# Modulation vectors for the third and fourth layer: from accumulating matmuls on TensorE to running sums on VectorE

## The chip, the cores and the metric

The kernel runs on one core of one Trainium2 chip. Its engines are TensorE (PE, with its weight loads as PEld), VectorE (DVE), ScalarE (ACT), GpSimd (POOL) and SyncE (SP), which issues the loads and stores here. Each engine works through its own list of instructions in order and waits at the head of the list. The metric is the device time of one execution in microseconds; lower is better.

## The reference

A stack of four layers works on 512 tokens (256 context tokens and 256 latent tokens) with 1,024 features in fp32. Each layer has a token mixer (gated DeltaNet, S5, RWKV-7, gated DeltaNet) and then a SwiGLU feed-forward network (FFN). Before each of them stands an RMSNorm whose result is shifted and scaled, and behind each a gate. These shifts, scales and gates are six vectors of 1,024 numbers per layer, made from the conditioning vector `c` (latent tokens) and from `c_ctx` (context tokens):

```
for each layer l, each part p of 6:
    mod[l, p] = silu(cond) @ mod_w[l][:, p] + mod_b[l, p]      # cond is c_ctx and c: two rows
h = rmsnorm(x, w) * (1 + scale) + shift
x = x + gate * mixer_or_ffn(h)
swiglu(h) = (silu(h @ w_in[:, :2816]) * (h @ w_in[:, 2816:])) @ w_out
```

One part takes a product of a 2 x 1,024 matrix with a 1,024 x 1,024 matrix of weights (4 MB), so the work is mostly that of reading the weights. Six parts per layer are 24 MB.

## The kernel before

**Layout.** Features lie on the 128 partitions in 8 blocks (`KD = 8`), tokens along the free dimension (`T = 512`), and the residual stream `X` stays on chip. Every large product is made of three matmuls (`mm3`, L134 to L138): weight and activation are both split into a high and a low part in a rounded fp32 form, `whi`, `wlo`, `hhi`, `hlo`. A weight tile comes in as `wraw` (256 KB, SP), ACT makes `whi` of it by a cast (L129), DVE makes `wlo = wraw - whi` (L130). Each of the three has four buffers (`weights`, `bufs=4`); a tile of 128 x 512 holds four blocks of 128, thus it serves 12 matmuls.

**The FFN** (`ffn`, L243) first runs `norm`: ACT squares `X`, DVE adds up `acc` (L197), one matmul with `ones` sums it over the partitions (L202), ACT makes the root (L203, L204), DVE multiplies (`t`, L219), ACT applies shift and scale (L227) and makes `hhi` (L159), and DVE makes `hlo` (L160). Then come 22 rounds `f` of two dense products of 24 matmuls each, `g` into a bank of `psd` and `u` into a bank of `psw`; ACT takes the SiLU of `g`, DVE multiplies it by `u` (L260), and the product is split into `fh` (ACT) and `fl` (DVE). Then come 8 output rows of 66 matmuls each, whose result DVE adds to `X` (`residual`, L239).

**The lanes.** The modulation vectors of the next layer are made inside the FFN of the layer ahead. A `Lane` (class at L1197) holds a generator and a rate; at each of 68 calls of `tick` (two in a round `f`, three in an output row) it is moved on by so many steps. `mods` (L163) has 8 steps per part: in step `k` two 256 KB tiles `mraw` are loaded (SP, L170, three buffers) and four matmuls follow (L172), with `cs` (128 x 32, in which two columns are in use) as weights and 256 columns of `mraw` as the moving operand; each goes to its own group of 32 partitions of the bank `psm`, and the 8 steps accumulate there. Then DVE copies the bank's half (L177), two transposes bring the vector onto the partitions (L180), and DVE adds the bias (L184). The lane takes 48 steps in 58 ticks. A second lane, `s5_prep`, runs in the first FFN alone.

**What sets the order.** The program is written in one order, but a scheduler that simulates the engines puts each engine's list into its final order when the kernel is built: work that is ready in its simulation is moved ahead of work that is not. So the ticks set a priority, and the place in an engine's list is only known from the built program.

Of the kernel before, what the change touches and what calls it, by code (L numbers as in the profile page):

```python
# [12 lines left out]
F32 = mybir.dt.float32  # L13
F32R = mybir.dt.float32r
AF = mybir.ActivationFunctionType
ALU = mybir.AluOpType
# [3 lines left out]
P = 128  # L20
T = 512
HALF = 256
KD = 8
# [4 lines left out]
class Net:  # L28
# [134 lines left out]
    def mods(self, l, parts, pool, raw):  # L163
        nc = self.nc
        for part in parts:
# [18 lines left out]
            nc.vector.tensor_tensor(dst, src, b, op=ALU.add)  # L184
            yield

    def raw_tile(self, pool, tag="mraw", bufs=4):
        return lambda: pool.tile([P, T], F32, name=self.nm(tag), tag=tag, bufs=bufs)

# [53 lines left out]
    def ffn(self, l, ts=slice(0, T), nxt=None):  # L243
        nc, tc = self.nc, self.tc
        with self.weights(), self.banks(w=4, m=2), self.open_h(), \
                tc.tile_pool(name=f"ffn{l}", bufs=1, reuse_waits="tile") as fp:
            if nxt is not None:
                self.lanes.append(Lane(self.mods(nxt, range(6), "m", self.raw_tile(fp, bufs=3)), 48, 58))
            if nxt == 1:
                self.lanes.append(Lane(self.s5_prep(fp, "m"), 130, 60))  # L250
            self.norm(l, 1, ts)
            hi, lo = [], []
            for f in range(NFFN):
                g = self.dense8(self.d["ffnin"][l, f, 0], ts)
                self.tick()
                u = self.dense8(self.d["ffnin"][l, f, 1], ts, pool="w")
                s = self.tmp()
                self.last_act = nc.scalar.activation(s[:, ts], g[:, ts], AF.Silu)
                a = self.tmp()
                nc.vector.tensor_tensor(a[:, ts], s[:, ts], u[:, ts], op=ALU.mult)  # L260
                ah = fp.tile([P, T], F32R, name=self.nm("fh"), tag=f"fh{f}")
                al = fp.tile([P, T], F32R, name=self.nm("fl"), tag=f"fl{f}")
                self.split(a[:, ts], ah[:, ts], al[:, ts])
                hi.append(ah)
                lo.append(al)
                self.tick()
            for f in range(KD):
                ps = self.ps("d")
                for k0 in range(0, NFFN, 8):
                    n = min(8, NFFN - k0)  # L270
                    w = self.wtile(self.d["ffnout"][l, f][:, k0 * P:(k0 + n) * P])
                    for i in range(n):
                        k = k0 + i
                        self.mm3(ps[:, ts], *w[i], hi[k][:, ts], lo[k][:, ts], k == 0, k == NFFN - 1)
                    self.tick()
                self.residual(l, 5, f, ps, ts)
            self.drain()
# [1588 lines left out]
```

## Time and profile before

| | |
|---|---|
| time, median of three runs | 3986.14 us (3984.36 to 4014.93) |
| the profiled execution: its time, its span | 3998.94 us, 3997.2 us |
| busy share of the span | PE 91%, PEld 70%, DVE 65%, ACT 51%, POOL 6% |
| granted clock of TensorE over the span | 0.928 of full speed |

The page gives busy time per engine, the chain of work that ended last (71% of it on PE), and groups of instructions by line of the kernel. A group names the output and inputs by the program's names, so `psm<-mraw,cs` is a matmul of a modulation step. The second FFN lies at about 1508 to 1931 us of the span and the third at about 2738 to 3153 us, in the trace's time axis; RWKV lies between them and the last GDN mixer behind the third. In a timeline the first number is the start, the second the duration. A matmul's record is longer than the distance to the next one's start, because matmuls are pipelined; what one costs is read from the starts. An fp32 matmul leaves two records, so that `x8` in an L172 row are four matmuls.

### The profile page before, as it was taken

To read this page: it belongs to the slowest core of one execution; us is meant where nothing else is said; L and a number is where in the kernel's file an instruction comes from. 1 tells how busy PE (TensorE), PEld (TensorE's weight loads), DVE (VectorE), ACT (ScalarE), POOL (GpSimd) and SP (SyncE) were. 2 spreads that over 40 slices of the span, in tenths; PEclk is the share of its full clock that TensorE was granted. 3 is DMA by queue.
4 is the path that set the end of the run, shared out by engine and by line. 5 is a ranking of instruction groups with operands and counts; after the bars stand their busy time and mean duration, and the time that the engine had idled before them with its cause. 6 is when DMAs were issued, how large, how long until landed. Compare 5 with 4: busy or idle time off the path is not lost.

```text
span 3997.2 us, 79365 instructions
## 1 busy us (share of the span) xinstructions
PE 3617.7 (91%) x30954; PEld 2803.3 (70%) x30954; DVE 2598.3 (65%) x6026; ACT 2053.7 (51%) x4533; POOL 238.9 (6%) x352
## 2 busy tenths in 40 slices
PE   6899999989999798999768999998999889998899
PEld 3676777757777686777546666675777667877798
DVE  6777888677776744333775677655332487888665
ACT  5666777553332334232454465544232467777654
POOL 0000000022322200000000000000000000000000
PEclk8999999989999898999877799868999898899899
DMA  5222111146665623444375456502444211121155
GB/s 194 93 83 80 49 46 49 46 127 192 201 213 179 240 86 124 156 154 144 131 274 199 143 197 210 185 12 95 156 155 157 71 54 44 61 64 61 57 178 161
DMA packets 266104, 511.62 MB, mean 128 GB/s; under 512 B 30464, under 2 KB 55680, under 8 KB 263296
## 3 DMA queue, kind: packets, MB, share of 16 engines
q1 hardware_dynamic: 265728, 506.55, 38.7%
q8 instruction: 243, 3.98, 0.4%
q14 instruction: 133, 1.09, 0.1%
HBM read 454.27 MB, written 52.17 MB: 127 GB/s over the span
## 4 chain that ended last, share of the span: by engine, by line
PE 71%; DVE 10%; ACT 9%; DMA 6%; issue 3%; SPq 0%; POOL 0%; DVEq 0%; ACTq 0%
PE psd L136 11%; PE psd L137 10%; PE psd L138 9%; PE psw L136 8%; PE psw L137 7%; PE psw L138 7%; PE psm L172 2%; DMA vx<-rw_x 2%; DMA mraw<-in_modw 2%; PE psi L530 2%; PE psw L1581 1%; PE psc L1390 1%; PE pso L1402 1%; PE psc L1407 1%; DMA wraw<-in_rwkv_rkv 1%
## 5 line engine op out<-in xcount | busy, mean ns | idle before, releaser
L129 ACT CAST whi<-wraw 128x512 fp32r<-128x512 f32 x854 | 521.5, 613 | 973.8 <-PE psd L137 553.6
L130 DVE TENSOR_TENSOR wlo<-wraw,whi 128x512 fp32r<-128x512 f32 x854 | 581.9, 683 | 643.6 <-ACT whi L129 629.1
L136 PE MATMUL psw<-hhi,whi 128*128 128x512 f32 (+1 forms) x1536 | 587.2, 382 | 19.3 <-ACT kT L372 6.5
L138 PE MATMUL psw<-hhi,wlo 128*128 128x512 f32 (+1 forms) x1536 | 570.9, 372 | 0.0
L137 PE MATMUL psw<-hlo,whi 128*128 128x512 f32 (+1 forms) x1536 | 570.8, 372 | 0.0
L136 PEld LDWEIGHTS psw<-hhi,whi 128*128 128x128 f32 x1536 | 296.2, 193 | 92.4 <-ACT whi L129 11.5
L138 PEld LDWEIGHTS psw<-hhi,wlo 128*128 128x128 f32 x1536 | 294.9, 192 | 50.5 <-issue 2.1
L137 PEld LDWEIGHTS psw<-hlo,whi 128*128 128x128 f32 x1536 | 295.6, 192 | 45.6 <-issue 2.5
L136 PE MATMUL psd<-hhi,whi 128*128 128x512 f32 (+1 forms) x784 | 296.7, 378 | 16.4 <-ACT hhi L159 16.4
L137 PE MATMUL psd<-hlo,whi 128*128 128x512 f32 (+1 forms) x784 | 290.3, 370 | 0.0
L138 PE MATMUL psd<-hhi,wlo 128*128 128x512 f32 (+1 forms) x784 | 289.1, 369 | 0.0
L136 PE MATMUL psd<-fh,whi 128*128 128x512 f32 (+1 forms) x704 | 261.4, 371 | 0.0
L137 PE MATMUL psd<-fl,whi 128*128 128x512 f32 (+1 forms) x704 | 257.4, 366 | 0.0
L138 PE MATMUL psd<-fh,wlo 128*128 128x512 f32 (+1 forms) x704 | 256.8, 365 | 0.0
L239 DVE SCALAR_TENSOR_TENSOR X<-psd,modT,X 128x256 f32<-128x256 f32 x376 | 166.6, 478 | 83.2 <-PE psd L138 81.0
L136 PEld LDWEIGHTS psd<-hhi,whi 128*128 128x128 f32 x784 | 149.4, 191 | 63.8 <-ACT hhi L159 19.8
L172 PE MATMUL psm<-mraw,cs 128*32 128x256 f32 x1280 | 139.2, 410 | 34.1 <-DMA mraw<-in_modw 21.7
L137 PEld LDWEIGHTS psd<-hlo,whi 128*128 128x128 f32 x784 | 149.0, 190 | 29.0 <-issue 2.9
L138 PEld LDWEIGHTS psd<-hhi,wlo 128*128 128x128 f32 x784 | 149.1, 190 | 24.1 <-issue 0.4
L136 PEld LDWEIGHTS psd<-fh,whi 128*128 128x128 f32 x704 | 132.9, 189 | 34.4 <-ACT whi L129 11.1
L137 PEld LDWEIGHTS psd<-fl,whi 128*128 128x128 f32 x704 | 133.0, 189 | 21.7 <-issue 1.6
L138 PEld LDWEIGHTS psd<-fh,wlo 128*128 128x128 f32 x704 | 133.0, 189 | 21.7
(537 smaller groups left out, 7778.9 us busy)
## 6 DMA issues: line engine op xcount, KB each, us to landing
mraw<-in_modw SPq DMA_DIRECT2D x384, 256.0 KB, 3.1
wraw<-in_ffnin SPq DMA_DIRECT2D x352, 256.0 KB, 2.8
vx<-rw_x SPq DMA_DIRECT2D x144, 512.0 KB, 4.7
wraw<-in_gdn_qkvz SPq DMA_DIRECT2D x192, 256.0 KB, 2.6
wraw<-in_ffnout SPq DMA_DIRECT2D x160, 256.0 KB, 2.8
wraw<-in_gdn_out SPq DMA_DIRECT2D x64, 256.0 KB, 2.6
wraw<-in_rwkv_rkv SPq DMA_DIRECT2D x48, 256.0 KB, 3.8
s5ca<-ca SPq DMA_DIRECT2D x32, 256.0 KB, 3.0
```

The costliest lines, as they stand in the source:

```text
L129: nc.scalar.copy(hi[:, :n], raw[:, :n])
L130: self.sub.tensor_tensor(lo[:, :n], raw[:, :n], hi[:, :n].bitcast(F32), op=ALU.subtract)
L136: mm(out, whi, ahi, start=start, stop=False)
L137: mm(out, whi, alo, start=False, stop=False)
L138: mm(out, wlo, ahi, start=False, stop=stop)
L172: nc.tensor.matmul(ps[64 * x + 32 * q:64 * x + 32 * q + 32, :256], self.cs[:, k, :], w[:, q * 256:q * 256 + 256], start=(k == 0), stop=(k ...
L239: nc.vector.scalar_tensor_tensor(self.X[:, f, c], ps[:, c], self.modT[l][:, gate, f, s:s + 1], self.X[:, f, c], op0=ALU.mult, op1=ALU.add)
L530: mm(o, x, y, start=True, stop=True)
L1390: mm(p, Z[:, dr * 8 + v * 4 + c], x, start=True, stop=True)
L1402: mm(oc, w, at[hd][:, cs], start=first, stop=(step % 2 == 1 and hd == 3))
L1407: mm(p, kd, w, start=True, stop=True)
L1581: mm(pg[h][:, c], BK[H[h], c0 + c, 64 * h:64 * h + 128], KR[H[h], c0 + c], start=True, stop=True)
```

## The change

In the second and third FFN (the vectors of layers 2 and 3) the lane `mods` is replaced by a new one, `mods_v`. The first FFN keeps `mods`. In `mods_v` one step loads one tile `mraw` (512 of the 1,024 columns) and DVE multiplies it by the conditioning value of each partition and adds it to a running sum, once for each of the two conditioning rows (`s`): the first of 8 tiles by a `tensor_scalar` (L200), the other seven by a `scalar_tensor_tensor` (L202). After 8 tiles two matmuls with a 128 x 32 block of ones (L207) sum the running sums over the partitions, 512 columns each. After both halves (`x`) ACT copies the bank (L210), four transposes follow (L213), and DVE adds the bias (L217). The lane takes 97 steps in 54 ticks and starts six ticks late.

```diff
+    def mods_v(self, l, parts, pool, raw, fp):
+        for part in parts:
+            ps = self.ps(pool)
+            for x in range(2):
+                sums = fp.tile([P, 2, T], F32, name=self.nm("msum"), tag="msum", bufs=2)
+                for k in range(KD):
+                    w = raw()
+                    nc.sync.dma_start(w, self.d["modw"][l, part, k][:, T * x:T * x + T])
+                    for s in range(2):
+                        c = self.cs[:, k, s:s + 1]
+                        if k == 0:
+                            nc.vector.tensor_scalar(sums[:, s], w, c, None, op0=ALU.mult)
+                        else:
+                            nc.vector.scalar_tensor_tensor(sums[:, s], w, c, sums[:, s], op0=ALU.mult, op1=ALU.add)
+                    if k < KD - 1:
+                        yield
+                for s in range(2):
+                    q = 64 * x + 32 * s
+                    nc.tensor.matmul(ps[q:q + 32], self.ones[:, 0:32], sums[:, s], start=True, stop=True)
+                yield
+            sb = self.tmp()
+            nc.scalar.copy(sb, ps)
+            pt = self.ps(pool)
+            for j in range(4):
+                nc.tensor.transpose(pt[:, j * P:j * P + P], sb[:, j * P:j * P + P], self.ident)
...
+            nc.vector.tensor_tensor(dst, src, b, op=ALU.add)
...
-                self.lanes.append(Lane(self.mods(nxt, range(6), "m", self.raw_tile(fp, bufs=3)), 48, 58))
+                raw = self.raw_tile(fp, bufs=3)
+                if nxt == 1:
+                    self.lanes.append(Lane(self.mods(nxt, range(6), "m", raw), 48, 58))
+                else:
+                    self.lanes.append(Lane(self.mods_v(nxt, range(6), "m", raw, fp), 97, 54, 6))
```

The new lines stand ahead of most of the kernel, so from `raw_tile` on each line has a number that is 32 higher, and from the FFN's rounds on 36 higher: L219 becomes L251, L260 becomes L296. Tile numbers shift too.

**DVE at the start of the second FFN.** Before, behind the last two additions into `acc`:

```order
L197 TENSOR_TENSOR acc<-acc,t_15946 128x512
L197 TENSOR_TENSOR acc<-acc,t_15949 128x512
L219 TENSOR_TENSOR t_15957<-X,acc 128x512
L219 TENSOR_TENSOR t_15963<-X,acc 128x512
L219 TENSOR_TENSOR t_15969<-X,acc 128x512
L219 TENSOR_TENSOR t_15975<-X,acc 128x512
L160 TENSOR_TENSOR hlo_15916<-t_15957,hhi_15908 128x512
```

and now (`msum` are the running sums):

```order
L229 TENSOR_TENSOR acc<-acc,t_15946 128x512
L202 SCALAR_TENSOR_TENSOR msum_16289<-mraw_16384,cs,msum_16289 128x512 x2
L229 TENSOR_TENSOR acc<-acc,t_15949 128x512
L202 SCALAR_TENSOR_TENSOR msum_16289<-mraw_16388,cs,msum_16289 128x512 x2
L202 SCALAR_TENSOR_TENSOR msum_16289<-mraw_16437,cs,msum_16289 128x512 x2
L202 SCALAR_TENSOR_TENSOR msum_16289<-mraw_16441,cs,msum_16289 128x512 x2
L202 SCALAR_TENSOR_TENSOR msum_16289<-mraw_16482,cs,msum_16289 128x512
L251 TENSOR_TENSOR t_15957<-X,acc 128x512
L251 TENSOR_TENSOR t_15963<-X,acc 128x512
L251 TENSOR_TENSOR t_15969<-X,acc 128x512
L251 TENSOR_TENSOR t_15975<-X,acc 128x512
L202 SCALAR_TENSOR_TENSOR msum_16289<-mraw_16482,cs,msum_16289 128x512
```

The scheduler has pulled the whole first part (16 tiles) up into the norm, in spite of the six ticks: six of the sums stand between the additions into `acc`, seven between the last of them and the first multiplication of the norm, and more between the `hlo`.

**DVE in a round of the second FFN.** Before, from one L260 to the next:

```order
L260 TENSOR_TENSOR t_16278<-t_16276,psw_16251 128x512
L130 TENSOR_TENSOR wlo_16337<-wraw_16335,whi_16336 128x512
L160 TENSOR_TENSOR fl_16281<-t_16278,fh_16280 128x512
L130 TENSOR_TENSOR wlo_16384<-wraw_16382,whi_16383 128x512
L130 TENSOR_TENSOR wlo_16390<-wraw_16388,whi_16389 128x512
L130 TENSOR_TENSOR wlo_16429<-wraw_16427,whi_16428 128x512
```

and now, in the third round, one of the fullest:

```order
L296 TENSOR_TENSOR t_16245<-t_16243,psw_16218 128x512
L202 SCALAR_TENSOR_TENSOR msum_16940<-mraw_16982,cs,msum_16940 128x512 x2
L130 TENSOR_TENSOR wlo_16302<-wraw_16300,whi_16301 128x512
L202 SCALAR_TENSOR_TENSOR msum_16940<-mraw_17031,cs,msum_16940 128x512
L160 TENSOR_TENSOR fl_16248<-t_16245,fh_16247 128x512
L202 SCALAR_TENSOR_TENSOR msum_16940<-mraw_17031,cs,msum_16940 128x512
L130 TENSOR_TENSOR wlo_16349<-wraw_16347,whi_16348 128x512
L202 SCALAR_TENSOR_TENSOR msum_16940<-mraw_17035,cs,msum_16940 128x512 x2
L130 TENSOR_TENSOR wlo_16355<-wraw_16353,whi_16354 128x512
L202 SCALAR_TENSOR_TENSOR msum_16940<-mraw_17076,cs,msum_16940 128x512 x2
L130 TENSOR_TENSOR wlo_16394<-wraw_16392,whi_16393 128x512
L202 SCALAR_TENSOR_TENSOR msum_16940<-mraw_17080,cs,msum_16940 128x512 x2
```

The same six instructions of the FFN now have ten of the lane among them. After such a burst of two half parts the next rounds have none, until the matmuls of L207 have freed the running sums, of which there are two buffers.

**PE between two dense products.** Before, a step of the lane:

```order
L138 MATMUL psd_16784<-hhi_15915,wlo_16780 128x512
L172 MATMUL psm_16522<-mraw_16809,cs 32x256 x2
L172 MATMUL psm_16522<-mraw_16813,cs 32x256 x2
L136 MATMUL psw_16829<-hhi_15908,whi_16818 128x512
L137 MATMUL psw_16829<-hlo_15916,whi_16818 128x512
```

and now a half part's end:

```order
L138 MATMUL psw_16901<-hhi_15915,wlo_16897 128x512
L207 MATMUL psm_16740<-msum_16741,ones 32x512 x2
L136 MATMUL psd_16957<-hhi_15908,whi_16946 128x512
L137 MATMUL psd_16957<-hlo_15916,whi_16946 128x512
L138 MATMUL psd_16957<-hhi_15908,wlo_16947 128x512
```

Where a step of four matmuls stood 48 times in an FFN, a pair of twice the columns stands 12 times; in both FFNs the first pair stands in the norm. Outside the two FFNs the program text is the same, but the scheduler's simulation reaches the later stages at other moments: in the RWKV mixer and in the last GDN mixer most matmuls stand at another place of PE's list (10 to 30 places away in the mean, up to some 150, when the matmuls of each form are paired in their order). The layers ahead of the second FFN are in the same order as before.

## Rows read from the trace of the kernel before

**Rows 1.** Busy time by stretch: stretch, length, PE, PEld, DVE, ACT, POOL, clock, DMA share, GB/s

```profile
1554.00:1931.00 377.00, 377.00 (x1832) 287.82 (x1830) 125.05 (x203) 105.37 (x176) 4.20 (x23) 1.00 0.43 137
2772.60:3153.00 380.40, 380.40 (x1863) 288.34 (x1861) 125.13 (x203) 105.64 (x177) 0.90 (x5) 1.00 0.43 140
...
1940.00:2730.00 790.00, 675.28 (x7855) 484.11 (x7856) 538.50 (x1323) 412.08 (x1048) 26.62 (x56) 0.81 0.49 167
3160.00:3790.00 630.00, 554.41 (x6574) 469.50 (x6574) 516.51 (x1374) 463.55 (x1094) 18.53 (x41) 0.92 0.17 56
```

**Rows 2.** Timeline of PE (start, duration, engine, line, operation), a full step of the lane

```profile
1613.95 0.39 PE L138 MATMUL psw<-hhi,wlo 128*128 128x512 f32 x1
1614.27 0.64 PE L172 MATMUL psm<-mraw,cs 128*32 128x256 f32 x8
1614.84 0.50 PE L136 MATMUL psd<-hhi,whi 128*128 128x512 f32 x1
1615.17 0.39 PE L137 MATMUL psd<-hlo,whi 128*128 128x512 f32 x1
1615.40 0.39 PE L138 MATMUL psd<-hhi,wlo 128*128 128x512 f32 x1
```

**Rows 3.** Timeline of PE, one matmul of the lane by itself

```profile
1541.52 0.62 PE L172 MATMUL psm<-mraw,cs 128*32 128x256 f32 x2
1542.07 0.50 PE L136 MATMUL psd<-hhi,whi 128*128 128x512 f32 x1
```

**Rows 4.** Instructions that read mraw, from 1554 to 1931 and from 2772.6 to 3153

```profile
L172 PE MATMUL psm<-mraw,cs x310: 379/390/404, 1608.0 to 1885.4; 128*32 128x256 f32 x155
...
L172 PE MATMUL psm<-mraw,cs x340: 378/392/404, 2799.3 to 3107.3; 128*32 128x256 f32 x170
```

**Rows 5.** Timeline of PE, two transposes of the lane; an fp32 matmul of 512 columns

```profile
1833.46 0.38 PE L180 MATMUL psm<-ident,t 128*128 128x128 f32 x2
1833.60 0.48 PE L136 MATMUL psd<-fh,whi 128*128 128x512 f32 x1
...
2317.42 1.13 PE L1632 MATMUL psw<-kd,bd 128*128 128x512 f32 x2
2318.47 0.27 PE L1716 MATMUL pso<-G,VS 128*64 128x64 f32 x1
```

**Rows 6.** Timeline of DVE, the nearest operation to the new sums

```profile
1965.33 2.73 DVE L1083 SCALAR_TENSOR_TENSOR t<-dx,rprm,hf 128x512 f32<-128x512 f32 x4
1967.98 0.68 DVE L160 TENSOR_TENSOR rlo<-t,rhi 128x512 fp32r<-128x512 f32 x1
```

**Rows 7.** Timeline of DVE, norm of the second FFN

```profile
1516.97 1.48 DVE L197 TENSOR_TENSOR acc<-acc,t 128x512 f32<-128x512 f32 x2
1523.87 2.50 DVE L219 TENSOR_TENSOR t<-X,acc 128x512 f32<-128x512 f32 x4 [5.41 <-ACT acc L204]
```

**Rows 8.** Timeline of PE, norm of the second FFN and a later point of it

```profile
1519.37 1.07 PE L172 MATMUL psm<-mraw,cs 128*32 128x256 f32 x4 [1.13 <-DMA mraw<-in_modw]
1520.37 2.08 PE L202 MATMUL psd<-acc,ones 128*128 128x512 f32 x2
...
1529.07 0.80 PE L136 MATMUL psd<-hhi,whi 128*128 128x512 f32 x1
...
1553.73 0.39 PE L138 MATMUL psw<-hhi,wlo 128*128 128x512 f32 x1
```

**Rows 9.** Timeline of PE, the same point of the third FFN

```profile
2772.49 0.39 PE L138 MATMUL psw<-hhi,wlo 128*128 128x512 f32 x1
```

**Rows 10.** Waits of SP's queue, 1560 to 1930; loads by line, to landing

```profile
SPq L128 <- DVE wlo L130: 206.4, 83, 5.9
...
mraw<-in_modw SPq DMA_DIRECT2D x384, 256.0 KB, 3.1
```

**Rows 11.** Groups by line: the cast of a weight tile on ACT and the subtraction on DVE

```profile
L129 ACT CAST whi<-wraw 128x512 fp32r<-128x512 f32 x854 | 521.5, 613 | 973.8 <-PE psd L137 553.6
L130 DVE TENSOR_TENSOR wlo<-wraw,whi 128x512 fp32r<-128x512 f32 x854 | 581.9, 683 | 643.6 <-ACT whi L129 629.1
```

## What is predicted, and from which rows

> **What bounds the kernel now.** The page comes first: TensorE is busy for 91% of the span and the chain of waits lies on it for 71%, so a matmul taken away can count, but only where PE is full. Which stretches are full is read from the table of windows [rows 1]. In both FFNs that change, PE is busy for the whole stretch behind the norm, 377.0 of 377.0 us and 380.4 of 380.4 us, at a granted clock of 1.00, while DVE works 125 us, a third of it. There a microsecond taken off PE's list is a microsecond off the span, and DVE has 250 us to spare. In the RWKV mixer and the last GDN mixer PE is idle for 115 of 790 and 76 of 630 us; nothing is taken from them.
>
> Next comes the timeline of PE inside a full stretch [rows 2]. Starts are to be read, not durations. A dense matmul with 512 columns starts 0.23 us ahead of the next (1615.17 to 1615.40), though its record is 0.39 us long. From 1613.95 to 1615.17 stand one dense matmul, a lane step of four matmuls, and one more dense matmul. Without the step the two would take 2 x 0.23, so the step costs 1.22 - 0.46 = **0.76 us**. From the step's own start to the next matmul's it is 0.57 us, and 0.55 us where one lane matmul stands alone [rows 3]. So the four run beside one another in their four column groups, and most of the price is paid once for a step.
>
> The instructions that read `mraw` give the number of steps [rows 4]: 310 and 340 records; eight records make a step of four matmuls. Counted in the timeline, with some steps split, they are 42 groups in the second FFN and 46 in the third. The rest of the 48 steps lie in the norm ahead of the stretch.
>
> **What is removed.** (42 + 46) x 0.76 = **66.9 us** of PE's time. The other way of reading it, records by their mean length, 310 x 0.390 + 340 x 0.392 = 254 us, is wrong, since the records overlap.
>
> A rule of the Trainium skill bears here (TensorEngine Tiling (Array Packing), Key Properties): tiles of the array work in parallel, and a change of tiling mode, not only of the tile, drains the engine. The trace agrees as far as 0.55 against 0.57 us go. The rule speaks against the change: what is removed was cheap, and by it alone a step costs a drain and not four streams. The sum by the rule and by the rows is the same 0.76 us a step, since that is the distance measured.
>
> **What is added on PE.** A pair of L207 stands 12 times in an FFN, the first time in the norm, so 11 times in the full stretch. The nearest row for a 512-column fp32 matmul is L1632 [rows 5]: 2317.42 to the next start at 2318.47, 1.05 us. That is 0.50 more than the 0.55 of a lane matmul with half the columns. The pair goes to two column groups, as the steps of before do, so I let the two run side by side and take the step's price with 0.50 added: 0.76 + 0.50 = **1.26 us**; 22 x 1.26 = 27.7 us. Lower bound: a pair costs no more than a step, 0.76 us (16.7 us). Upper bound: the two run one behind the other, 1.05 us more (22 x 2.31 = 50.8 us). The value lies at the lower end because both old rows show groups side by side. Four transposes in place of two: two take 0.14 us [rows 5], twelve parts, 1.7 us. Steady sum: 66.9 - 27.7 - 1.7 = **37.5 us** gained.
>
> **What is added on DVE.** The nearest operation to the new sums is L1083, a scalar_tensor_tensor of the same 128 x 512 with a per-partition scalar [rows 6]: four of them from 1965.33 to 1967.98, 0.66 us each. Twelve half parts x 2 rows x 7 = 168 of them in an FFN, 111 us, and 24 tensor_scalar, which no row shows at this size. Those I bound by nothing and 0.66, and take at 0.4, 10 us (an estimate: one tensor input instead of two). DVE goes from 125 to about 240 us in a stretch of some 358 us. On the average it stays hidden. In the fullest round, shown above, ten sums and six operations of the FFN stand together: 10 x 0.66 + 6 x 0.61 = 10.3 us, against 48 dense matmuls x 0.227 = 10.9 us on PE. Still hidden, but hardly.
>
> What waits for DVE there is PE, through `wlo` (L130). A tile of weights serves 12 matmuls, 2.7 us. With four buffers of each kind, a tile can be made three tiles ahead, 8.2 us. Of that, the cast takes 0.61 and the subtraction 0.68 us [rows 11]; **6.9 us** are left for which L130 may be late. A pair of sums ahead of it takes 1.3 us, so the sums as such don't reach PE. A sum that must wait for its tile does more: DVE takes its list in order, and everything behind it, L130 above all, waits too. A tile of `mraw` lands 3.1 us behind its issue, and its issue can stand on SP behind a weight load that waits for a free buffer, at worst 5.9 us [rows 10], in 83 such waits of 206.4 us. 3.1 + 5.9 = 9.0 us, 2.1 us beyond the slack. Below: no stall, as three buffers of `mraw` let the loads run ahead; above: 2.1 us at each half part, 22 x 2.1 = 46 us. I take the low end, 1.5 us in all: before, the same loads ran through the same three buffers and PE, which took them in order too, lost nothing by it in the full stretches [rows 1].
>
> **The norm.** In the second FFN six sums stand between the additions into `acc` (the last two from 1516.97 to 1518.45) [rows 7] with a tensor_scalar pair ahead, in all about 4.5 us. PE's L202 came at 1520.37 [rows 8], 1.9 us behind the additions, as PE was first held by an L172 that waited 1.13 us for its tile; now it comes at about 1523. Seven sums stand ahead of the first L219, 4.6 us; it moves from 1523.87 to about 1528, and the first dense matmul from 1529.07 to about 1533. But of the 384 records of a lane 384 - 310 = 74 lay ahead of the full stretch [rows 4], some eight groups of them behind 1529, and none of those is left: 8 x 0.6 = 5 us less against 4 us late, so the last dense matmul ahead of the full stretch, 1553.73 before, comes at about 1553. In the third FFN fewer sums stand ahead of the first `hlo`, fewer groups go too, and I take the same 1 us off 2772.49 [rows 9]. Together **2 us** gained, between 8 lost (4 us twice, nothing caught up) and 8 gained (the groups go, and no delay reaches PE).
>
> **The sum.** -37.5 - 2 + 1.5 = **-38 us**. The profiled execution took 3998.94 us (span 3997.2), so 3961 of its kind. It lies 12.8 us above the median of the runs, 3986.14; the same 38 us off the median give **3948 us**, 0.95% less. About 1% is what a measurement of this kernel can tell from no change: below 3946 counts as faster, above 4026 as slower.
>
> **The rivals.**
> 1. The two L207 of a pair run one behind the other: 22 x 1.05 = 23 us, 3971. For it: L1632, on the whole array, shows 1.05 us for one, and no row has two of 512 columns in one step. Against it: [rows 2 and 3], where four cost what one costs.
> 2. DVE's order holds PE (the other side). The place is a sum that stands ahead of L130 and waits for `mraw` while SP is held by a weight load. At 2.1 us in each of 22 half parts, 46 us: 3994, no gain. The gain is gone at 38 / 22 = 1.7 us a half part. From 38 + 40 = 78 us on, 3.5 us a half part, it is slower than before by over 1%; two such waits in each half part (4.2 us, 92 us) give 4040. For it: the sums come in bursts of two half parts, 16 tiles in some three rounds, where the steps came evenly; in the fullest round DVE has 0.6 us left of 10.9. Against it: the loads are issued three tiles ahead, and DMA is busy for 0.43 of the stretch only [rows 1].
> 3. The other order in the RWKV and the last GDN mixer. PE is idle there for 191 us together; if the new order moves 5% of that (an estimate), it is 10 us either way: 3938 or 3958.
> 4. The norm's delay is not caught up: 8 us lost in place of 2 gained, 3958.
>
> **How the numbers follow.** The forecast, with small stalls, 0.5: 3935 to 3961 for the errors of the pair's price and of the norm (rival 4 among them), of which about 45% lie below 3946. Rival 1, 0.1. Rival 2 at one wait a half part 0.13, at two 0.07. Rival 3, gain 0.1, loss 0.1. Faster: 0.5 x 0.45 + 0.1 for rival 3, and 0.02 for more than that = 0.35. Slower: 0.07. Same: 0.58. The range from 3922 (pairs at 0.76, 11 us, and mixers at their best, 10 us, with some of the norm) to 3980 leaves out the two-wait case and most of the one-wait case, 0.17, and little below.
>
> **What would show it.** In the profile after: a pair of L207 from its start to the next dense start about 1.05 us (2.1 if rival 1 holds). The full stretches shorter by 18 to 20 us each, 377 to about 358, with PE busy for the whole. DVE busy 240 us in them. Idle time of DVE that ends with an `mraw` load, and of PE that ends with L130 of DVE, would show rival 2. First dense matmul of the second FFN 4 us later. RWKV at 790 and the last GDN at 630 us, with rival 3 the difference. Wrong above all would be the step's price, if the dense matmuls beside the pairs run at another pitch than 0.23, or DVE's price, if a sum on a fresh tile takes longer than 0.66 us: at 0.75 the fullest round takes 11.2 us, more than PE's 10.9.

## The result

The changed kernel took 3955.2 us in the median of six runs (3936.94 to 3967.57) against 4003.54 us of the kernel before, also in six. The medians lie 48 us apart; the ratio is put at 0.9893, with a 95% interval of 0.987 to 0.9915, thus 1.1% or some 43 us less. The forecast was 38 us less. Two repetitions further down gave 0.9859 and 0.9847, 56 and 61 us less. The time lies inside the range of 3922 to 3980. Which side of the 1% line it is on stays open: the ratio lies just on the faster side, to which the prediction gave 0.35, but its interval reaches across the line; in microseconds the time lies above the 3946 that the prediction drew there, since the kernel before took 17 us more in these six runs than in the three that it started from.

**The profile after.** The table of windows of the changed kernel, for the full stretches of the second and third FFN and for the two mixers, is cut at about the same points of the program as [rows 1] (columns as there):

```profile
1554.70:1913.10 358.40, 358.40 (x1578) 286.20 (x1576) 220.10 (x358) 111.25 (x187) 4.26 (x23) 1.00 0.47 147
2751.80:3110.20 358.40, 358.40 (x1578) 286.22 (x1576) 224.73 (x366) 111.53 (x187) 3.02 (x16) 1.00 0.47 148
1922.10:2709.70 787.60, 682.45 (x7856) 484.98 (x7857) 539.30 (x1321) 412.49 (x1050) 26.72 (x56) 0.81 0.49 167
3117.70:3758.00 640.30, 559.16 (x6574) 472.54 (x6574) 519.06 (x1375) 465.97 (x1095) 19.69 (x41) 0.91 0.17 55
```

PE is still busy for the whole of both full stretches, at clock 1.00. They are 18.6 and 22.0 us shorter than in [rows 1] (18.7 and 21.4 when both ends are taken at the same matmuls, as further down). DVE went from 125 to 220 and 225 us of busy time, less than the 240 of the forecast, because 36 and 27 of the 192 sums of an FFN ran ahead of these stretches. PE waited for DVE nowhere in them.

The ones-matmul of each norm marks where a stage begins. In the timeline of PE of the kernel before (the first of them stands in [rows 8], at 1520.37) the ones behind the second FFN, behind RWKV, behind the third FFN and behind the last GDN are:

```profile
1933.60 0.67 PE L202 MATMUL psd<-acc,ones 128*128 128x512 f32 x1 [2.45 <-DVE acc L197]
2740.68 1.19 PE L202 MATMUL psd<-acc,ones 128*128 128x512 f32 x1 [3.65 <-DVE acc L197]
3155.54 0.67 PE L202 MATMUL psd<-acc,ones 128*128 128x512 f32 x1 [2.45 <-DVE nega L325]
3789.39 0.70 PE L202 MATMUL psd<-acc,ones 128*128 128x256 f32 x2 [1.56 <-DVE acc L197]
```

and in the timeline of PE of the changed kernel, from the second FFN's on:

```profile
1525.35 2.08 PE L234 MATMUL psd<-acc,ones 128*128 128x512 f32 x2 [14.63 <-DVE acc L229]
...
1915.68 1.32 PE L234 MATMUL psd<-acc,ones 128*128 128x512 f32 x2 [2.45 <-DVE acc L229]
...
2720.36 1.19 PE L234 MATMUL psd<-acc,ones 128*128 128x512 f32 x1 [3.64 <-DVE acc L229]
...
3113.21 1.10 PE L234 MATMUL psd<-acc,ones 128*128 128x512 f32 x2 [2.85 <-DVE acc L229]
...
3757.43 0.70 PE L234 MATMUL psd<-acc,ones 128*128 128x256 f32 x2 [1.59 <-DVE acc L229]
```

The distances between such starts, in us, here and in every experiment (its kernel is named by what it does below; "2nd" and so on is which execution of the same program). The last column is the granted clock of TensorE over the RWKV stage:

| kernel | first GDN | 1st FFN | S5 | 2nd FFN | RWKV | 3rd FFN | last GDN | last FFN | clock, RWKV |
|---|---|---|---|---|---|---|---|---|---|
| before | 830.4 | 466.1 | 210.6 | 413.2 | 807.1 | 414.9 | 633.9 | 198.9 | 0.81 |
| before, 2nd | 831.0 | 465.7 | 211.8 | 414.3 | 808.9 | 414.9 | 632.3 | 199.4 | 0.81 |
| changed | 835.1 | 463.4 | 213.3 | 390.3 | 804.7 | 392.9 | 644.2 | 198.9 | 0.81 |
| changed, 2nd | 833.4 | 464.2 | 212.7 | 390.4 | 794.5 | 394.2 | 639.4 | 198.8 | 0.83 |
| changed, 3rd | 835.2 | 462.9 | 214.5 | 390.3 | 783.7 | 394.1 | 639.3 | 198.9 | 0.84 |
| quad4 | 831.8 | 466.6 | 213.2 | 384.4 | 805.9 | 388.3 | 637.2 | 198.7 | 0.82 |
| late | 834.4 | 463.0 | 209.9 | 390.0 | 798.3 | 390.3 | 643.8 | 198.9 | 0.82 |
| lane_out | 832.5 | 463.4 | 208.9 | 370.0 | 803.4 | 370.6 | 636.7 | 199.4 | 0.82 |
| double | 830.8 | 462.1 | 215.3 | 396.8 | 800.4 | 399.5 | 633.2 | 199.6 | 0.82 |
| only_third | 826.8 | 463.8 | 210.2 | 414.1 | 803.3 | 394.5 | 632.4 | 198.9 | 0.81 |
| late_quad | 828.8 | 470.9 | 209.0 | 382.7 | 785.2 | 383.5 | 639.6 | 199.0 | 0.84 |
| late_quad, 2nd | 831.0 | 467.1 | 208.2 | 381.5 | 797.3 | 383.4 | 636.7 | 198.9 | 0.83 |
| triple | 832.6 | 466.1 | 216.2 | 522.6 | 815.7 | 537.8 | 639.0 | 199.6 | 0.82 |

In the profiled executions the two FFNs are 22.9 and 22.0 us shorter, S5 (with the start of the norm behind it) 2.7 longer, RWKV 2.4 shorter and the last GDN 10.3 longer. Ahead of the change, where both kernels have the same order, the first GDN is 4.7 us longer and the first FFN 2.7 shorter.

### The profile page after: what moved, and what is told of

It is laid out like the page before. It is cut to its first block, busy times and chain, and to the rows that moved or that the text cites. A ratio compares the mean times of both kernels' runs of the same rounds, so it can differ in the third digit from the quotient of the medians.

```text
span 3965.8 us, 78603 instructions
## 1 busy us (share of the span) xinstructions
PE 3580.5 (90%) x30306; PEld 2805.2 (71%) x30306; DVE 2830.9 (71%) x6398; ACT 2061.8 (52%) x4545; POOL 243.6 (6%) x352
## 4 chain that ended last, share of the span: by engine, by line
PE 71%; DVE 12%; ACT 9%; DMA 5%; issue 3%; SPq 1%; POOL 0%; DVEq 0%; ACTq 0%
PE psd L136 10%; PE psd L137 10%; PE psd L138 9%; PE psw L136 7%; PE psw L137 7%; PE psw L138 7%; DMA vx<-rw_x 2%; PE psw L1617 2%; PE psi L566 2%; DMA mraw<-in_modw 2%; PE psc L1426 1%; PE pso L1438 1%; ACT whi L129 1%; ACT E L430 1%; PE psc L1443 1%
## 5 line engine op out<-in xcount | busy, mean ns | idle before, releaser
L130 DVE TENSOR_TENSOR wlo<-wraw,whi 128x512 fp32r<-128x512 f32 x854 | 581.7, 683 | 412.4 <-ACT whi L129 404.8
L202 DVE SCALAR_TENSOR_TENSOR msum<-mraw,cs,msum 128x512 f32<-128x512 f32 x336 | 236.6, 744 | 2.9 <-DMA mraw<-in_modw 2.7
L136 PEld LDWEIGHTS psd<-hhi,whi 128*128 128x128 f32 x784 | 149.4, 191 | 66.5 <-ACT hhi L159 29.1
```

The lines of the kernel that those rows point to most:

```text
L130: self.sub.tensor_tensor(lo[:, :n], raw[:, :n], hi[:, :n].bitcast(F32), op=ALU.subtract)
L136: mm(out, whi, ahi, start=start, stop=False)
L202: nc.vector.scalar_tensor_tensor(sums[:, s], w, c, sums[:, s], op0=ALU.mult, op1=ALU.add)
```

## The experiments

**Both programs again.** No edit; how much does a stage differ between two executions of one program, and is the last GDN's loss that?

> The kernel before, unchanged, profiled once more. It measures how much a stage's length differs between two executions of one program. Ratio 1.000, interval within 0.4%. In the first profiles the last GDN mixer (from one norm's ones-matmul to the next) took 633.9 us before and 644.2 us after, 10.3 us more. Theory A (the length of a mixer varies by that much from one execution to another): the last GDN comes out anywhere in 630 to 645 us here too, and the first GDN, whose order is the same in both kernels, varies by 4 us or more (830.4 and 835.1 so far). Rival B (the other order of the matmuls costs 10 us): 634 us again within 2 us. The FFNs, being full of matmuls at clock 1.00, come out within 1 us of 413.2 and 414.9 us by either.

> The changed kernel, unchanged, profiled once more. Ratio 0.987 to 0.992. The second and third FFN 390.3 and 392.9 us within 1 us. Theory A: the last GDN anywhere in 630 to 645 us. Rival B: 644 us again within 2 us.

Measured: ratios 0.9998 (0.9983 to 1.0014) and 0.9859 (0.9837 to 0.988), the second just below what I expected. The FFNs repeat within 1.4 us. The last GDN took 632.3 us with the order of before and 639.4 with the new one, and 639.3 in a third execution: neither theory in full. Three executions with the new order lie 5 to 12 us above the two with the old. That the order is the cause is not shown: the first GDN, whose instructions stand in the same order in both kernels, took 833.4 to 835.2 us in the changed kernel and 830.4 and 831.0 before, and 826.8 to 835.2 over all the kernels of the table. RWKV is another matter: 804.7, 794.5 and 783.7 us with one and the same program. Here are the windows of RWKV for the first and the third of them (first the changed kernel, then its third execution):

```profile
1915.70:2720.40 804.70, 689.51 (x7875) 488.43 (x7875) 554.56 (x1353) 423.54 (x1069) 26.72 (x56) 0.81 0.49 167
```

```profile
1916.30:2700.00 783.70, 667.15 (x7874) 471.75 (x7875) 553.80 (x1353) 423.38 (x1069) 26.78 (x56) 0.84 0.51 171
```

The same work takes 21 us less; PE's busy time falls by 22 us, and the granted clock is 0.84 in place of 0.81. Over the whole table RWKV goes with that clock: 803 to 809 us at 0.81, 798 to 806 at 0.82 (with triple, 816, as the one exception), 795 and 797 at 0.83, 784 and 785 at 0.84. So RWKV's length says little about an order when it comes from one profile.

**lane_out: the ceiling.**

```diff
-                    self.lanes.append(Lane(self.mods_v(nxt, range(6), "m", raw, fp), 97, 54, 6))
+                    for part in range(6):
+                        b = self.modb[:, nxt, part].unsqueeze(2).to_broadcast([P, KD, 2])
+                        nc.vector.tensor_copy(self.modT[nxt][:, part], b)
```

> Leaves out the modulation vectors of layers 2 and 3 (they are set to the bias alone): no loads of their weights, no sums, no lane matmuls in the second and third FFN. It is the ceiling of what taking the lane off TensorE can give. By the step's price of 0.76 to 0.79 us and the 88 groups of the full stretches, the old lane cost 67 to 70 us there; the FFNs, 413.2 and 414.8 us before, come out at about 413 - 32 - 2 = 377 to 380 and 415 - 36 - 2 = 376 to 379 us (the 2 us for the groups in the norm). By it the changed kernel, with 390.4 and 392.8 us, paid 11 x 1.18 + 2 = 15 us each for pairs and transposes and nothing for DVE. Rival (DVE's sums hold PE a little all along): the FFNs come out below 374 us, more than 16 us under the changed kernel's. The mixers: RWKV 794 to 809, last GDN 632 to 644 us, with another order again.

Measured: 0.9763 (0.9723 to 0.9803); FFNs 370.0 and 370.6 us, 5 to 10 below what I expected, and below the 374 that I had taken for the sign of the rival. So the old lane cost 43 and 44 us in an FFN, not 34 to 38, and the new one costs 20 and 22. Where the missing part lay shows when the FFN is cut at its 75th dense matmul. In the timeline of PE of lane_out that matmul and the next norm are, first in the second and then in the third FFN,

```profile
1545.55 0.39 PE L138 MATMUL psw<-hhi,wlo 128*128 128x512 f32 x1
...
1890.43 1.10 PE L234 MATMUL psd<-acc,ones 128*128 128x512 f32 x2 [2.45 <-DVE acc L229]
...
2719.10 0.39 PE L138 MATMUL psw<-hhi,wlo 128*128 128x512 f32 x1
...
3064.43 1.10 PE L234 MATMUL psd<-acc,ones 128*128 128x512 f32 x2 [2.90 <-DVE acc L229]
```

that is, in the second FFN, 344.9 us for the full stretch with the end of the FFN, and 25.2 from the norm's ones-matmul (1520.37) to it. Before, the same two are 379.9 (1553.73 to 1933.60) and 33.4. The full stretch paid 35.0 us for the lane, 42 groups at about 0.8 us with the transposes; the norm paid another 8.2, more than I had thought it held. In the changed kernel (75th dense matmul at 1554.46) they are 361.2 and 29.1: 16.3 and 3.9 us are left. The rival of a steady small hold by DVE has no room: 11 pairs at 1.18 us make 13.0 of those 16.3, and six groups of four transposes at 0.45 us make 2.7, which leaves 0.6 us. Such a group in the timeline of PE of the changed kernel, 0.91 us from the dense matmul ahead to the second one behind it, less 2 x 0.23:

```profile
1631.15 0.40 PE L138 MATMUL psd<-hhi,wlo 128*128 128x512 f32 x1
1631.39 0.60 PE L213 MATMUL psm<-ident,t 128*128 128x128 f32 x4
1631.75 0.48 PE L136 MATMUL psw<-hhi,whi 128*128 128x512 f32 x1
1632.06 0.40 PE L137 MATMUL psw<-hlo,whi 128*128 128x512 f32 x1
```

**quad4: one group of four ones-matmuls for a part.**

```diff
-            ps = self.ps(pool)
+            ps, held = self.ps(pool), []
...
-                sums = fp.tile([P, 2, T], F32, name=self.nm("msum"), tag="msum", bufs=2)
+                sums = fp.tile([P, 2, T], F32, name=self.nm("msum"), tag="msum", bufs=4)
...
-                for s in range(2):
-                    q = 64 * x + 32 * s
-                    nc.tensor.matmul(ps[q:q + 32], self.ones[:, 0:32], sums[:, s], start=True, stop=True)
+                held.append(sums)
                 yield
+            for q in range(4):
+                nc.tensor.matmul(ps[32 * q:32 * q + 32], self.ones[:, 0:32], held[q // 2][:, q % 2], start=True, stop=True)
```

> One change to the changed kernel: the four ones-matmuls of a part (two halves, two conditioning rows) are issued as one group behind the second half, with four buffers of running sums in place of two. Theory (groups in four column groups cost what one matmul costs, and each microsecond off PE in the full stretch counts): a group of four costs 1.18 us as a pair does now, six in place of twelve per FFN, 5 or 6 x 1.18 = 6 to 7 us less in each FFN, 384 and 386 us, 12 to 14 us less than the changed kernel, a ratio to the kernel before of about 0.986. Rival (matmuls of a group run partly one behind the other): a group of four costs 2.2 us or more, and nothing is gained. Second rival (longer bursts on DVE, four half parts in a row, hold the split of the weights): PE is idle in the full stretch before matmuls that read wlo, and the FFNs are no shorter than 390 us.

Measured: 0.9871 (0.9853 to 0.9889); FFNs 384.4 and 388.3 us, 6.0 and 4.6 to 5.9 less than the changed kernel's. Timelines of PE, a pair in the changed kernel and a group of four in quad4 (x4 and x8 records):

```profile
1647.97 0.39 PE L138 MATMUL psw<-hhi,wlo 128*128 128x512 f32 x1
1648.29 1.05 PE L207 MATMUL psm<-msum,ones 128*32 128x512 f32 x4
1649.27 0.50 PE L136 MATMUL psd<-hhi,whi 128*128 128x512 f32 x1
1649.61 0.39 PE L137 MATMUL psd<-hlo,whi 128*128 128x512 f32 x1
```

```profile
1675.05 0.39 PE L138 MATMUL psd<-hhi,wlo 128*128 128x512 f32 x1
1675.37 1.06 PE L208 MATMUL psm<-msum,ones 128*32 128x512 f32 x8
1676.37 0.50 PE L136 MATMUL psw<-hhi,whi 128*128 128x512 f32 x1
1676.70 0.39 PE L137 MATMUL psw<-hlo,whi 128*128 128x512 f32 x1
```

From the dense matmul ahead to the second one behind it is 1.64 and 1.65 us; less 2 x 0.23 that is 1.18 and 1.19 us. Two more matmuls cost 0.01 us. The theory of the groups holds, though the FFNs give 5 or 6 us where I expected 6 to 7: five groups fewer stand in the full stretch of the second FFN, and four fewer in the third, where two matmuls of the first part stand singly. PE waits for nothing from 1560 to 1900, which rules out the second rival. The whole time shows nothing of it beside the changed kernel (0.9871 and 0.9859): some 11 us in the FFNs are less than what RWKV differs by from one execution to another.

**late: no sum in the norm.** The conditioning values come from a copy that reads the last `hlo` of the norm.

```diff
+        cv = fp.tile([P, KD, 2], F32, name=self.nm("cv"), tag="cv")
+        nc.vector.scalar_tensor_tensor(cv, self.hlo[KD - 1][:, 0:16].bitcast(F32).rearrange("p (k s) -> p k s", s=2), 0.0,
+                                       self.cs[:, :, 0:2], op0=ALU.mult, op1=ALU.add)
...
-                        c = self.cs[:, k, s:s + 1]
+                        c = cv[:, k, s:s + 1]
```

> One change to the changed kernel: the running sums take their conditioning values from a copy that needs the last hlo tile of the norm, so that no sum can stand in the norm on DVE. Theory (the sums in the norm make the first dense matmul about 5 us late): in the second FFN it comes 6 to 8.7 us behind the norm's ones-matmul, which itself comes 3 to 5 us earlier; the FFNs come out 2 to 4 us shorter together with the stage ahead of them, since the first part's two pairs (2.4 us) and its 16 tiles now lie in the full stretch; ratio about 0.988. Rival (DVE catches up later and the delay costs nothing): no stage is shorter, 390 and 393 us, or longer by the two pairs.

Measured: 0.9875 (0.9852 to 0.9898). S5 with the norm's start 209.9 us, 2.8 to 4.6 less; second FFN 390.0, unchanged; third 390.3, 2.6 to 3.9 less. In the timeline of PE the ones-matmul and the first dense matmul of late are

```profile
1520.66 2.08 PE L237 MATMUL psd<-acc,ones 128*128 128x512 f32 x2 [10.06 <-DVE acc L232]
1527.52 0.79 PE L136 MATMUL psd<-hhi,whi 128*128 128x512 f32 x1 [4.78 <-ACT hhi L159]
```

where the changed kernel had 1525.35 and 1535.00:

```profile
1530.08 1.91 PE L207 MATMUL psm<-msum,ones 128*32 128x512 f32 x2 [2.66 <-DVE msum L202]
1533.15 1.92 PE L207 MATMUL psm<-msum,ones 128*32 128x512 f32 x2 [1.16 <-DVE msum L202]
1535.00 0.80 PE L136 MATMUL psd<-hhi,whi 128*128 128x512 f32 x1
```

The sums made the ones-matmul 4.6 us late (PE waited 14.63 us for DVE there, in late 10.06), and the first pair of L207, each half of it waiting for its sum, stood ahead of the first dense matmul as well. Cut at the 75th dense matmul, the second FFN of late takes 26.5 us from the ones-matmul to it, where the changed kernel takes 29.1, and 363.5 us behind it, where that takes 361.2. One more pair stands in the full stretch, twelve in place of eleven and not two as I had expected, which is 1.2 of these 2.3 us; the rest is not traced. So the second FFN gives back what it won in its norm, and the gain is that of S5 ahead of it; in the third the norm wins 5.0 us and the stretch gives back 2.4. The theory holds, at some 3 to 4 us for an FFN with the stage ahead of it. The whole time does not show it beside the changed kernel.

**late_quad: both edits.** 

> Both edits together: the four ones-matmuls of a part in one group, and no sum in the norm. If the parts add: FFNs of 384.4 - 0 to 2 = 382 to 385 and 388.3 - 2.5 = 385 to 388 us and S5 with the norm's start at 210 us, some 12 us less in these stages than the changed kernel. The whole time 3,930 to 3,945 us on the scale of the changed kernel's 3,948, a ratio to the kernel before of 0.982 to 0.986, if the mixers don't take it back; their order is a new one again, worth up to 10 us either way.

> The kernel with both edits once more, unchanged. The first time its RWKV mixer took 785.2 us, where the kernel before took 807.1 and 808.9 and the changed kernel 804.7 and 794.5. Theory A (the order that this program has in RWKV is a faster one): 785 us again within 4 us. Theory B (one program's RWKV differs by 10 us and more from one execution to another, by the granted clock): it comes out between 785 and 805 us, and the granted clock of the stretch moves with it. The FFNs 382.7 and 383.5 us within 1.5 us by either. Ratio to before 0.980 to 0.986.

Measured: 0.9817 (0.9792 to 0.9843), and once more 0.9828 (0.98 to 0.9856), beside a ratio of 0.9847 (0.9822 to 0.9872) for the changed kernel run beside the second. FFNs 382.7 and 383.5, then 381.5 and 383.4; S5 209.0 and 208.2: about 23 us less than the changed kernel in these three stages, where I had expected 12 and the parts as measured above give 17. RWKV was 785.2 and then 797.3 us, at a granted clock of 0.84 and 0.83: theory B again. It is the fastest of the kernels here that compute all, 1.7 to 1.8% under the kernel before, though its interval and that of the changed kernel overlap.

> The changed kernel a third time, beside the one with both edits, so that both have their time on one chip. FFNs 390 and 393 us within 1.5 us; RWKV 790 to 805, last GDN 638 to 645 us. Ratio to before 0.985 to 0.990, and to the kernel with both edits above 1.002, if the 17 us that this one is shorter by in the FFNs and in S5 hold.

FFNs 390.3 and 394.1 us and last GDN 639.3, as expected; RWKV, at 783.7, fell below what I gave it, and so, by a little, did the ratio. Against the kernel with both edits the two ratios give 1.002, which is no more than the limit I had set, and their intervals overlap: the gain of both edits is shown in the stages and not in the whole time.

**only_third: the change in the third FFN alone.**

```diff
-                if nxt == 1:
+                if nxt < 3:
```

> The change in the third FFN alone; the second keeps the accumulating matmuls, and the RWKV mixer keeps the order of before (the last GDN has an order of its own). Additive theory: FFNs 413 to 414.5 and 392 to 394 us. Mixers: if the order in RWKV gave the changed kernel something, RWKV is 807 to 809 us here, as in both profiles of before, against 804.7 and 794.5; if it is only the granted clock that differs from one execution to another, it can come out anywhere between. If the last GDN's 5 to 10 us are the price of an order that differs from the one of before, they are here in some measure too; if they belong to the order of the changed kernel alone, 632 to 634 us. Ratio about 0.994 to 0.997.

Measured: 0.9932 (0.991 to 0.9954), a little better than expected; FFNs 414.1 and 394.5 us, so the two FFNs add. RWKV with the order of before took 803.3 us here, inside the spread of the changed kernel: no gain of the new order is shown there. The last GDN, in a third order, took 632.4, so not every new order comes with the 5 to 12 us; in the other kernels of the table, each with an order of its own, it took 633 to 644.

**double and triple: how far DVE can be loaded.** Behind each scalar_tensor_tensor one more, or two more, into a scratch tile.

```diff
+        dump = fp.tile([P, T], F32, name=self.nm("dump"), tag="dump")
+        nc.vector.memset(dump, 0.0)
...
                             nc.vector.scalar_tensor_tensor(sums[:, s], w, c, sums[:, s], op0=ALU.mult, op1=ALU.add)
+                            nc.vector.scalar_tensor_tensor(dump, w, c, dump, op0=ALU.mult, op1=ALU.add)
```

> Each of the 168 scalar_tensor_tensor sums of an FFN is followed by a second one into a scratch tile that nobody reads: 168 x 0.66 = 111 us more of DVE in each FFN, 222 + 111 = about 333 of some 360 us of the full stretch. Theory (in the changed kernel DVE's work is hidden with room on the average, but the fullest round, 10.2 of PE's 10.9 us, is at the edge): now the fullest round takes about 10 x 0.66 more, 17 us, PE waits for wlo in each burst, DVE is busy for over 85% of the stretch, and the FFNs come out 10 to 50 us longer than 390 and 393 us; the gain of 21 to 23 us per FFN is gone or more. Rival (the buffers smooth the bursts): FFNs within 3 us of 390 and 393, DVE about 333 us busy.

Measured: 0.9904 (0.9881 to 0.9926); FFNs 396.8 and 399.5 us. Windows of double:

```profile
1560.00:1900.00 340.00, 340.00 (x1470) 266.96 (x1469) 312.68 (x502) 102.80 (x174) 0.52 (x2) 1.00 0.50 155
2780.00:3090.00 310.00, 310.00 (x1345) 243.87 (x1344) 288.18 (x464) 91.23 (x154) 1.77 (x5) 1.00 0.50 157
```

DVE is busy for 92 and 93% and PE does not wait at all. The FFNs are 6 us longer all the same: behind the 75th dense matmul of the second FFN the ones-matmuls now stand in 16 groups in place of 11, single ones where the second row's sum comes later, and five more at 1.18 us are 5.9 us. A single one costs what a pair does:

```profile
1642.83 0.39 PE L137 MATMUL psw<-hlo,whi 128*128 128x512 f32 x1
1643.15 1.04 PE L210 MATMUL psm<-msum,ones 128*32 128x512 f32 x2
1644.12 0.50 PE L138 MATMUL psw<-hhi,wlo 128*128 128x512 f32 x1
1644.46 0.39 PE L136 MATMUL psw<-hhi,whi 128*128 128x512 f32 x1
```

By the number neither theory is met (10 to 50 us longer, or within 3). By the mechanism the first is wrong and the rival right: a round that asks more of DVE than PE takes is smoothed by the buffers.

> Two scratch sums behind each of the 168 sums of an FFN. With one, DVE was busy for 92% of the full stretch and PE lost nothing by waiting. Now DVE's work is about 338 + 111 = 450 us in each FFN against some 367 us of PE. Theory (DVE bounds as soon as its work exceeds PE's): the FFNs come out at 440 to 460 us, DVE is busy for over 97% and PE waits for wlo of L130. Rival (the lane only falls behind, and what is left of it is done behind the FFN's last dense matmul): the FFN stays near 397 to 410 us to its end, and what follows starts late by the rest. Second rival (PE is held earlier, as soon as single bursts exceed a round): the FFNs are longer than 470 us, with DVE idle at times.

Measured: 1.0631 (1.0596 to 1.0667); the second FFN took 522.6 us (ones-matmul at 1528.8 and at 2051.4), the third 537.8. That is more than 470, the figure of the second rival, but its reason (single bursts hold PE) is not what the trace shows. Waits of PE from 1529 to 2052 (what waited for what, us in total, times, longest):

```profile
PE psm L211 <- DVE msum L204: 106.0, 4, 31.1
PE psd L238 <- DVE acc L233: 25.3, 2, 17.4
PE psd L136 <- ACT hhi L159: 6.0, 1, 6.0
```

PE is held, but not by `wlo`: it stands at the ones-matmul of the lane (L211 here), up to 31.1 us for one, until the last sum has come, with the dense matmuls behind it in its queue. The first of these waits begins at 1765. The windows up to it and behind it:

```profile
1560.00:1765.00 205.00, 205.00 (x882) 161.41 (x880) 190.21 (x298) 63.13 (x107) 0.00 (x0) 1.00 0.43 137
1765.00:2040.00 275.00, 167.69 (x689) 127.84 (x688) 250.66 (x388) 44.14 (x74) 5.67 (x23) 0.79 0.34 105
```

For 205 us PE runs full with DVE at 93%, so single bursts don't hold it; then the lane has fallen so far behind that PE meets its matmul too early. Behind these waits PE also runs at a lower granted clock, 0.79 in the mean of that window. DVE stays near 91% while PE idles, as it waits now and then for `mraw` (25.8 us in 48 waits in this FFN), whose buffers it frees itself.

## Why the prediction was right, and where not

**What bounds the kernel** was right. All that left PE in the full stretches left the span, and DVE's 95 to 100 us more in them cost nothing that the runs show (0.6 us are left unexplained, see lane_out).

**The sum** was 37.5 us in the full stretches. Cut at the 75th dense matmul the second FFN gained 379.9 - 361.2 = 18.7 us. In the third, the 75th stands at 2772.49 [rows 9] and 2751.59 with the next ones-matmul at 3155.54 and 3113.21, 383.05 against 361.62, a gain of 21.4. Together 40.1. That is 2.6 us more than forecast. The terms follow from lane_out, whose stretches take 344.9 and 345.3 us: the old lane cost 35.0 and 37.7 us in them, the new one 16.3 and 16.3. Twelve groups of two transposes at 0.24 us come off the one, twelve of four at 0.45 off the other, 2.6 us apart where the forecast had 1.7. What is left makes 0.79 us for each of the 88 steps and not 0.76 (3.0 us more removed), and 1.24 for each of the 22 pairs and not 1.26 (0.5 us less added). Read from the starts around it, a step costs 0.77 and a pair 1.18 us; part of the few hundredths beyond that lies in the next dense matmuls, which start 0.23 us apart behind a group of the changed kernel, where 0.227 is the usual distance. Taking the price from one quiet place (1613.95 to 1615.17) was good to 5%. Rival 1, pairs one behind the other, is out: 0.98 us from a pair's start to the next dense one, and 1.00 from a group of four's, and 0.97 from a single one's.

**The record-length reading**, 254 us for both FFNs, would have missed the 72.7 us that lane_out shows (35.0 and 37.7) by a factor of 3.5.

**The norm** came out right in sum, in part by luck. I said L202 at 1523 and the first dense matmul at 1533; they came at 1525.35 and 1535.00, of which the stages ahead explain 2.2 us. The seven sums and the first multiplication of the norm stand in the timeline of DVE, the first `hhi` in that of ACT:

```profile
1525.21 4.82 DVE L202 SCALAR_TENSOR_TENSOR msum<-mraw,cs,msum 128x512 f32<-128x512 f32 x7
1529.94 2.49 DVE L251 TENSOR_TENSOR t<-X,acc 128x512 f32<-128x512 f32 x4
```

```profile
1532.65 0.60 ACT L159 CAST hhi<-t 128x512 fp32r<-128x512 f32 x1
```

Without these 2.2 us L251 came at 1527.7, where I said 1528. What I missed is that the first pair of L207 stands ahead of the first dense matmul and waits there for its sums, 2.66 and 1.16 us: `hhi` was ready at 1533.25, the dense matmul began at 1535.00. And the old groups cost more in the norm (8.2 us) than the 5 that I took. The two misses have opposite signs: the 75th came at 1554.46, 0.7 later than before where I said 0.7 earlier, or 1.5 earlier without the 2.2 us. The touched stages gave 22.9 + 22.0 - 2.7 = 42.2 us, the full stretches 40.1 of them; the 2.1 that are left are the 2 of the forecast.

**DVE's stalls** I put at 1.5 us. There was one in the second FFN, ahead of the full stretch, in the timeline of PE of the changed kernel:

```profile
1545.26 0.50 PE L138 MATMUL psd<-hhi,wlo 128*128 128x512 f32 x1 [1.00 <-DVE wlo L130]
```

SP was held by the weight loads as before (up to 5.9 us, as [rows 10]), yet DVE waited for `mraw` only 1.7 us from 1500 to 1913; the waits of DVE there are

```profile
DVE wlo L130 <- ACT whi L129: 97.8, 58, 3.2
DVE t L296 <- PE psw L138: 18.8, 13, 1.6
...
DVE msum L202 <- DMA mraw<-in_modw: 1.3, 3, 0.6
DVE msum L200 <- DMA mraw<-in_modw: 0.4, 1, 0.4
```

Rival 2 had the right danger and the wrong place. No load kept DVE for more than 0.6 us, and L130 does not keep PE even where DVE is busy for 92% (double). What did make a kernel slower is the matmul on PE that waits for a lane that has fallen behind. That sets in somewhere between the load of double and that of triple; the busy share of DVE doesn't tell it, since both show 92 to 93%. The price of a sum was right: 0.744 us long, 0.66 from start to start.

**The mixers**: the size of rival 3 was right, 5 to 12 us lost in the last GDN, but that its order is the cause is not shown, since the first GDN differs by 3 to 5 us between the same two kernels without another order. RWKV's 2 to 25 us less can't be put down to order either, since one program's RWKV spreads over 21 us and goes with the granted clock. Why that clock differs from execution to execution, and what costs the last GDN its time, stays open; no run here tells it. That these two stages also moved the ratio from 0.9893 to 0.9859 and 0.9847 is likely but not shown, as only one run of each set was profiled.

**The chances** put the time within 1% at 0.58. The stages that the change touches gave 42.2 us, 1.05%, where the forecast had 38: 2.6 of the difference lie in the full stretches, by the price of a step above all, and 1.5 are the stalls that did not come there. The 1% line lay 2 us from the forecast, closer than these terms were known.

## What to carry to other kernels

Price a group of small matmuls by the distance of the starts around it, in a stretch that is full, and count groups rather than matmuls: four cost here what one does, so what pays is fewer groups. When work goes from a full engine to a half-empty one, ask what the full engine will still wait for: here not the instructions that share the other's queue, but the one matmul that collects the result, and its place in the queue must be far enough behind. And cut a profile into stages before judging a change of 1%: a stage of this kernel differed by 21 us between two executions of one program.

## What the runs showed of the hardware

Matmuls of 32 columns in different column groups ran side by side at both lengths: from start to next start 0.55 us for one of 256 moving columns and 0.57 for four [rows 2, 3], 0.97 us for one of 512 (double, 1643.15 to 1644.12), 0.98 for two (1648.29 to 1649.27) and 1.00 for four (1675.37 to 1676.37). That agrees with the Trainium skill, TensorEngine Tiling (Array Packing), Key Properties, by which tiles work independently.

In the norm of the changed kernel, behind 14.63 us in which PE was idle, its granted clock was at the lower of its two levels (1.2 of 2.4 GHz):

```profile
1525.00:1536.00 11.00, 6.84 (x8) 1.70 (x9) 10.99 (x19) 6.65 (x13) 0.00 (x0) 0.50 0.43 139
```

The record of one matmul of L207 is 1.91 us long there, that of a pair in the full stretch 1.05. Work moved into such a gap is not free when dense matmuls queue behind it: here the first of them began 1.75 us after its input was ready.
